# Softmax weights times values in a two-layer decoder trunk: one head at a time over the full width of TensorE, or four heads in a row in the two halves of its columns

## The chip, the core and the metric

The kernel runs on one core of one Trainium2 chip. The metric is device time in microseconds, the median of several executions; lower is better. A profile is taken of one further execution.

## What is computed

A decoder trunk of two layers over 256 tokens with 1024 features, batch 1, all in float32. A layer adds to the stream a mixer of three branches, and then a squared-ReLU MLP with 4096 hidden features:

```python
for l in range(DEPTH):                       # 2
    h = rms_norm(x, attn_norm[l])
    x = x + hybrid_mixer(h, ...)             # MLA, MoBA, retention, gated and merged
    h = rms_norm(x, mlp_norm[l])
    x = x + squared_relu_mlp(h, w_mlp_up[l], w_mlp_down[l])
return rms_norm(x, final_norm)
```

Two of the branches are causal softmax attention with 8 heads, a value dimension of 64 and 256 positions (MoBA's block is as long as the sequence, so only its own causal block remains):

```python
s = jnp.einsum('bhqd,bhkd->bhqk', qb, k) * scale
s = jnp.where(kpos[None, :] <= qpos[:, None], s, NEG_INF)
p = jax.nn.softmax(s, axis=-1)
o = jnp.einsum('bhqk,bhkd->bhqd', p, v)      # the product that the change is about
```

## The kernel before

Tokens are worked on in two tiles of 128. Large products are made from split operands: a value is cut into a rounded part and a rest (`whi`/`wlo` for weights, `xs`, `omlah`/`omlal` and so on for activations), and `three` (L209 to L212) makes three products of them. Weights come in pieces of at most 512 KB over SyncE's queue into four `raw` buffers; ScalarE makes `whi` (L190), VectorE `wlo` (L191).

A layer is a list of units, `prog`: projections, gates, branch products. `at(slot, step)` hangs a further step behind the unit with that number, and `run` goes through the list. What comes of it is the program order; a scheduler then orders each engine's instructions by its own simulated times, except within `tc.manual_schedule`, where the named engine keeps the order in which the code gives them. Engines take their instructions strictly in order.

The attention (`attention`, L433, and `attention_head`, L390) is spread over these slots so that its small steps lie between the large products. Head `h` has three steps: `scores` in slot `first + h`, `turn` two slots later, and `values` three slots later.

- `scores`: query times key into the bank `ps_s`, mask and maximum on VectorE, exponentials on ScalarE, division on VectorE. The result is `prob`, 128 queries by 128 keys and 128 queries by 256 keys. The fourth block of 128x128 is empty by causality and is never made.
- `turn`: three 128x128 transposes on TensorE into `ps_pt` (L421), and a copy on ScalarE to `probT` (L423), which has two buffers: keys on the partitions, queries along the row.
- `values`: two products into `po`, key tile 0 for all 256 queries (L428) and key tile 1 for the last 128 (L429). The stationary operand is 128 columns of the values, which are two heads' 64 columns side by side, so of the 128 rows of the result only the 64 of the head at hand are used.

Two heads share a bank `po`, in its two halves of 256 columns. Behind the odd head's `values`, `out` takes the two useful quarters, rows 0 to 63 of the even head and rows 64 to 127 of the odd one, and splits each with `split_plain`: a copy on ScalarE (L229) and a subtraction on VectorE (L230), 64x256 each. The targets are `omlah`/`omlal` in the MLA branch and `omobah`/`omobal` in the MoBA branch, `oT` in the code, with chunk `i` for the heads `2i` and `2i + 1`. The units `bmla` and `bmoba` multiply them with the branch weights later.

The PSUM banks of `po`, `ps_s`, `ps_pt` and several others come from one pool of four (`misc_tile`). The score products and `values` are plain float32. The values are `vml` in the MLA branch and `mv` in the MoBA branch.

Of the kernel before, what the change touches and what calls it, by code (L numbers as in the profile page):

```python
# [7 lines left out]
F32 = mybir.dt.float32  # L8
# [5 lines left out]
P = 128  # L14
D = 1024
S = 256
# [10 lines left out]
MLA_H, MLA_QR, MLA_KVR, NOPE, ROPE, VD = 8, 256, 128, 64, 32, 64  # L27
QKD = NOPE + ROPE
MB_H, MB_D = 8, 64
# [96 lines left out]
def trunk(ctx: ExitStack, tc: tile.TileContext, x, wts, consts, gains, gfin, xtok, out):  # L126


    nc = tc.nc
# [4 lines left out]
    sb = ctx.enter_context(tc.tile_pool(name="sb", bufs=1))  # L134
# [65 lines left out]
    def misc_tile(name="misc"):  # L200
        return ps.tile([P, 512], F32, name=name, tag="misc", bufs=4)
# [18 lines left out]
    def small(name):  # L220
        return sb.tile([P, 8], F32, name=name, tag="st", bufs=12)
# [6 lines left out]
    def split_plain(src, hi, lo):  # L228
        nc.scalar.activation(hi, src, AF.Copy)  # L229
        nc.vector.tensor_sub(lo, src, hi.bitcast(F32))  # L230
# [154 lines left out]
    def stacked_scores(parts, o, qs, ks, swap=False):  # L385
        for i, (q, k) in enumerate(parts):
            a, b = q[:, qs], k[:, ks]
            nc.tensor.matmul(o, b if swap else a, a if swap else b, start=i == 0, stop=i == 1)  # L388

    def attention_head(o, score, vs, scale):  # L390


        got = {}

        def scores():
            s_ps = misc_tile("ps_s")
            score(s_ps[:, 0:P], slice(0, P), slice(0, P))
            score(s_ps[:, P : 3 * P], slice(P, S), slice(0, S))
            p = sb.tile([P, 3 * P], F32, name="prob", bufs=3)
            m = small("smx")  # L400
            nc.vector.tensor_tensor_reduce(
                p[:, 0:P], s_ps[:, 0:P], mask[:, P : 2 * P], 1.0, NEG_INF, ALU.add, ALU.max, m[:, 0:1]
            )
            nc.vector.tensor_tensor_reduce(
                p[:, P : 3 * P], s_ps[:, P : 3 * P], mask, 1.0, NEG_INF, ALU.add, ALU.max, m[:, 1:2]
            )
            nc.vector.tensor_scalar(m[:, 2:4], m[:, 0:2], -scale, None, op0=ALU.mult)  # L407
            spans = ((0, P), (P, 3 * P))
            for i, (a, b) in enumerate(spans):
                nc.scalar.activation(  # L410
                    p[:, a:b], p[:, a:b], AF.Exp, bias=m[:, 2 + i : 3 + i], scale=scale, accum_out=m[:, 4 + i : 5 + i]
                )
            nc.vector.reciprocal(m[:, 6:8], m[:, 4:6])
            for i, (a, b) in enumerate(spans):
                nc.vector.tensor_scalar(p[:, a:b], p[:, a:b], m[:, 6 + i : 7 + i], None, op0=ALU.mult)
            got["p"] = p

        def turn():
            pt = misc_tile("ps_pt")
            for i, src in enumerate((0, P, 2 * P)):  # L420
                nc.tensor.transpose(pt[:, P * i : P * i + P], got["p"][:, src : src + P], ident)  # L421
            pT = sb.tile([P, 3 * P], F32, name="probT", bufs=2)
            nc.scalar.activation(pT, pt[:, : 3 * P], AF.Copy)  # L423
            got["pT"] = pT

        def values():
            dst, v, pT = o(), vs(), got["pT"]
            nc.tensor.matmul(dst, v[0], pT[:, 0:S], start=True, stop=False)  # L428
            nc.tensor.matmul(dst[:, P:S], v[1], pT[:, S : 3 * P], start=False, stop=True)  # L429

        return scores, turn, values

    def attention(oT, score, vs, scale, first):  # L433


        o_ps = {}

        def o_of(h):
            if h % 2 == 0:
                o_ps[h // 2] = misc_tile("po")  # L440
            return o_ps[h // 2][:, S * (h % 2) : S * (h % 2) + S]

        def out(h):
            i = h // 2
            for j in range(2):
                rows = slice(64 * j, 64 * j + 64)
                split_plain(o_ps[i][rows, S * j : S * j + S], oT[0][rows, i, :], oT[1][rows, i, :])

        for h in range(8):
            steps = attention_head(  # L450
                lambda h=h: o_of(h), lambda o, qs, ks, h=h: score(h, o, qs, ks), lambda h=h: vs(h), scale
            )
            for lag, step in zip((0, 2, 3), steps):
                at(first + h + lag, step)
            if h % 2:
                at(first + h + 3, lambda h=h: out(h))

    def gates(l, key, xn):

# [49 lines left out]
    prog, steps = [], {}  # L509

    def at(slot, step):
        steps.setdefault(slot, []).append(step)

    def slot(key, j):
        return [k for k, _ in prog].index((key, j))
# [9 lines left out]
    def layer(l, xn, before):  # L525

        c0 = []
        c, mla, mqkv, rqkv = {}, {}, {}, {}
# [133 lines left out]
        first = slot("mv", 3)  # L662
        at(first, lambda: omlaT.extend((t4("omlah"), t4("omlal"))))

        def mla_score(h, o, qs, ks):
            nc.tensor.matmul(o, mla["Q"][:, h, qs], mla["K"][:, h, ks], start=True, stop=True)  # L666

        attention(
            omlaT, mla_score,
            lambda h: [v[:, P * (h // 2) : P * (h // 2) + P] for v in mla["v"]], QKD**-0.5, first,  # L670
        )


# [4 lines left out]
        first = slot("gmla1", 3)  # L678
# [12 lines left out]
        for i in range(4):  # L691
            at(first + 2 * i - 1, lambda i=i: moba_turn(i))
        attention(
            omobaT,
            lambda h, o, qs, ks: stacked_scores(qkT[h // 2][h % 2], o, qs, ks),
            lambda h: [v[:, P * (h // 2) : P * (h // 2) + P] for v in mqkv["mv"]], MB_D**-0.5, first,
        )


# [163 lines left out]
        def up(f, between=None):  # L863

            u = misc_tile("pup")
            if f >= NF - WHOLE:
                project_t(l, "up", f, xm, u[:, 0:S])
                return u
            wh, wl = load_w(l, "up", f, 0)
            for k in range(KD):  # L870
                if between and k in between:
                    between[k]()
                nc.tensor.matmul(u, wh[:, k, :], xm.both(k), start=k == 0, stop=False)  # L873
                nc.tensor.matmul(u[:, 0:S], wl[:, k, :], xm.k(k)[0], start=False, stop=k == KD - 1)  # L874
            return u
# [35 lines left out]
        first = [up(f, {1: {4: lambda: xm.stats(accs[3])}, 2: {4: xm.stats_row}}.get(f)) for f in range(LAG + 1)]  # L911
# [20 lines left out]
        if not last:  # L932
# [7 lines left out]
            def turned(q):  # L940
                t, half = quarters[q]
                pt = misc_tile("pyd")
                for i in range(4):
                    nc.tensor.transpose(pt[:, P * i : P * i + P], ys[q][:, P * i : P * i + P], ident)
                x_t = X[half][:, :, P * t : P * t + P]
                nc.vector.tensor_add(x_t, x_t, pt.rearrange("p (k s) -> p k s", k=4))
                xn.take_part(t, half)
# [18 lines left out]
        for t in range(NT):  # L966
            for half in range(2):
                q, cs = 2 * t + half, slice(512 * half, 512 * half + 512)
# [22 lines left out]
    for i, (k, n) in enumerate(b0_units(0)):  # L991
# [4 lines left out]
        tag, bufs = ("t4", T4) if n == 2 else ("w2k", W2K)  # L996
# [22 lines left out]
    for l in range(L):  # L1019
        xn, before = layer(l, xn, before)  # L1020
# [85 lines left out]
```

## Time and profile before

| | us |
|---|---|
| median of 3 executions | 861.49 (861.37 to 861.53) |
| profiled execution | 861.24 |
| its span, first to last instruction of the program | 859.5 |
| TensorE busy (products) | 849.2 |
| TensorE busy (loads of weights) | 728.8 |
| VectorE busy | 618.1 |
| ScalarE busy | 507.7 |

In a row of the profile, PE is TensorE's product, PEld its load of weights, DVE VectorE, ACT ScalarE and SP SyncE. "L428" is the line of the kernel, `po<-probT,vml` the tile written and the tiles read. "128*128" is the part of TensorE's array that a product takes, "128x256" partitions by columns of its result, and "x32" the number of records. A timeline row has the start, the time to the end of the last of its records, and their number. A PE record lasts until its modelled end, so records overlap: what a product costs a full TensorE is the time from its start to the next start. A windows row has the stretch, then the busy time of PE, PEld, DVE, ACT and POOL with instruction counts, the granted clock, and the DMA engines' share and GB/s.

### The profile page before, as it was taken

Reading aid. Unit: us, or ns where it says so; the run is one execution under the profiler, and the core shown is the slowest. Engines: PE = TensorE matmul, PEld = TensorE weight load, DVE = VectorE, ACT = ScalarE, POOL = GpSimd, SP = SyncE. Lnnn points to the kernel's source line nnn. Section 1 sums busy time; section 2 is a strip of 40 time slices with the busy share of each in tenths; the row PEclk is TensorE's granted clock in tenths of the full one; section 3 lists DMA queues with packets and bytes.
Section 4 is the critical chain, followed back from the end, with each engine's and each line's share of the span. In section 5 each row is a group of like instructions: output and inputs, shape, how many; then the busy total and the mean of one; then the engine's idle time right before and its main releaser. Section 6 shows DMA issues by size and latency. Waiting matters only on the chain.

```text
span 859.5 us, 12496 instructions
## 1 busy us (share of the span) xinstructions
PE 849.2 (99%) x4544; PEld 728.8 (85%) x4544; DVE 618.1 (72%) x1198; ACT 507.7 (59%) x885; POOL 12.1 (1%) x23
## 2 busy tenths in 40 slices
PE   8999999999999999999999999999999999999997
PEld 7888888988898888888888888889889988888885
DVE  6896787787777666666589767977877776666664
ACT  7766776535456555555577567665355565555553
POOL 0000000000000000000000000000100000000000
PEclk9999999999999999999999999999999999999999
DMA  9775344446366665555356455445565666666641
GB/s 339 235 233 172 124 147 140 148 155 194 126 196 195 202 192 192 183 188 192 109 202 213 153 159 163 139 140 168 150 194 148 174 205 191 190 182 185 196 123 50
DMA packets 42541, 150.08 MB, mean 175 GB/s; under 512 B 4848, under 2 KB 5360, under 8 KB 42480
## 3 DMA queue, kind: packets, MB, share of 16 engines
q1 hardware_dynamic: 42192, 149.13, 55.7%
q8 instruction: 36, 0.59, 0.3%
q10 hardware_dynamic: 288, 0.16, 0.1%
q14 instruction: 25, 0.20, 0.1%
HBM read 148.22 MB, written 1.05 MB: 174 GB/s over the span
## 4 chain that ended last, share of the span: by engine, by line
PE 96%; DVE 1%; ACT 1%; issue 1%; DMA 1%; SPq 0%; POOLq 0%; POOL 0%; ACTq 0%
PE acc L210 22%; PE acc L211 22%; PE acc L212 22%; PE pup L873 13%; PE pup L874 7%; PE po L428 2%; PE ps_s L666 1%; PE ps_pt L421 1%; PE ps_s L388 1%; PE po L429 1%; DMA raw<-wts 1%; ACT whi L190 0%; PE pqk L686 0%; DVE wlo L191 0%; PE ps_r L388 0%
## 5 line engine op out<-in xcount | busy, mean ns | idle before, releaser
L191 DVE TENSOR_TENSOR wlo<-raw,whi 128x1024 fp32r<-128x1024 f32 (+2 forms) x279 | 336.3, 1209 | 164.2 <-ACT whi L190 162.3
L190 ACT ACTIVATE whi<-raw 128x1024 fp32r<-128x1024 f32 (+2 forms) x279 | 292.0, 1048 | 257.7 <-PE acc L212 152.0
L873 PE MATMUL pup<-xs,whi 128*128 128x512 f32 x496 | 176.9, 398 | 0.0
L211 PE MATMUL acc<-wlo,xs 128*128 128x512 f32 (+1 forms) x384 | 151.8, 395 | 0.6 <-DVE wlo L191 0.6
L210 PE MATMUL acc<-whi,xs 128*128 128x512 f32 (+1 forms) x384 | 150.7, 397 | 0.4 <-ACT whi L190 0.3
L212 PE MATMUL acc<-whi,xs 128*128 128x512 f32 (+1 forms) x384 | 150.7, 393 | 0.0
L874 PE MATMUL pup<-xs,wlo 128*128 128x256 f32 x496 | 138.3, 280 | 0.0
L873 PEld LDWEIGHTS pup<-xs,whi 128*128 128x128 f32 x496 | 92.9, 188 | 21.3
L210 PE MATMUL acc<-whi,sq 128*128 128x512 f32 x256 | 101.5, 397 | 0.4 <-ACT sq L229 0.4
L211 PE MATMUL acc<-wlo,sq 128*128 128x512 f32 x256 | 100.0, 391 | 0.0
L212 PE MATMUL acc<-whi,sq 128*128 128x512 f32 x256 | 99.5, 393 | 0.0
L874 PEld LDWEIGHTS pup<-xs,wlo 128*128 128x128 f32 x496 | 93.6, 189 | 2.2
L210 PEld LDWEIGHTS acc<-whi,xs 128*128 128x128 f32 x384 | 72.2, 188 | 14.3 <-ACT whi L190 1.5
L211 PEld LDWEIGHTS acc<-wlo,xs 128*128 128x128 f32 x384 | 72.3, 188 | 14.1 <-DVE wlo L191 1.6
L212 PEld LDWEIGHTS acc<-whi,xs 128*128 128x128 f32 x384 | 72.3, 188 | 13.0
L212 PEld LDWEIGHTS acc<-whi,sq 128*128 128x128 f32 x256 | 47.9, 188 | 11.7 <-DVE sq L230 0.2
L210 PEld LDWEIGHTS acc<-whi,sq 128*128 128x128 f32 x256 | 48.0, 188 | 11.2 <-ACT sq L229 0.8
L211 PEld LDWEIGHTS acc<-wlo,sq 128*128 128x128 f32 x256 | 48.2, 188 | 8.8
L211 PE MATMUL acc<-mTl,whi 128*128 128x256 f32 x128 | 36.3, 284 | 1.0 <-DVE mTl L230 1.0
L210 PE MATMUL acc<-mTh,whi 128*128 128x256 f32 x128 | 36.2, 285 | 0.0
L212 PE MATMUL acc<-mTh,wlo 128*128 128x256 f32 x128 | 36.1, 283 | 0.0
L410 ACT ACTIVATE prob<-prob,smx 128x128 f32<-128x128 f32 x64 | 28.3, 445 | 7.5 <-DVE smx L407 7.2
(241 smaller groups left out, 1196.3 us busy)
## 6 DMA issues: line engine op xcount, KB each, us to landing
raw<-wts SPq DMA_DIRECT2D x268, 512.0 KB, 3.7
raw<-wts SPq DMA_DIRECT2D x7, 416.0 KB, 3.3
xrow<-xtok SPq DMA_DIRECT2D x4, 256.0 KB, 8.4
y<-y SPq DMA_DIRECT2D x4, 256.0 KB, 2.2
DEC<-consts SPq DMA_DIRECT2D x1, 768.0 KB, 7.5
x<-x SPq DMA_DIRECT2D x1, 512.0 KB, 6.3
raw<-wts SPq DMA_DIRECT2D x2, 256.0 KB, 3.7
gf<-gfin SPq DMA_DIRECT2D x1, 512.0 KB, 3.9
```

What stands on the lines that cost most here:

```text
L190: nc.scalar.activation(hi[:, :sz], raw[:, :sz], AF.Copy)
L191: nc.vector.tensor_sub(lo[:, :sz], raw[:, :sz], hi[:, :sz].bitcast(F32))
L210: nc.tensor.matmul(o, ah, bh, start=start, stop=False)
L211: nc.tensor.matmul(o, ah, bl, start=False, stop=False)
L212: nc.tensor.matmul(o, al, bh, start=False, stop=stop)
L388: nc.tensor.matmul(o, b if swap else a, a if swap else b, start=i == 0, stop=i == 1)
L410: nc.scalar.activation(p[:, a:b], p[:, a:b], AF.Exp, bias=m[:, 2 + i : 3 + i], scale=scale, accum_out=m[:, 4 + i : 5 + i])
L421: nc.tensor.transpose(pt[:, P * i : P * i + P], got["p"][:, src : src + P], ident)
L428: nc.tensor.matmul(dst, v[0], pT[:, 0:S], start=True, stop=False)
L429: nc.tensor.matmul(dst[:, P:S], v[1], pT[:, S : 3 * P], start=False, stop=True)
L873: nc.tensor.matmul(u, wh[:, k, :], xm.both(k), start=k == 0, stop=False)
L874: nc.tensor.matmul(u[:, 0:S], wl[:, k, :], xm.k(k)[0], start=False, stop=k == KD - 1)
```

## The change

`values` is no longer a step of one head. It runs once for four heads, behind the third slot after the last of them; `scores` and `turn` stay per head, where they were. `probT` has five buffers instead of two. `values` takes a bank `po` and makes eight products in it, under `manual_schedule` for TensorE: first the pair of heads 2 and 3 of the four, then heads 0 and 1, and in a pair the odd head and the even one by turns, key tile 0 and then key tile 1. The stationary operand is now the head's own 64 columns. The odd head's result goes to partitions 64 to 127, the even head's to 0 to 63, so a pair fills a half of the bank, 256 columns, and four heads fill it. One `split_plain` over 128x512 then takes the bank to two chunks of `oT`.

```diff
-            pT = sb.tile([P, 3 * P], F32, name="probT", bufs=2)
+            pT = sb.tile([P, 3 * P], F32, name="probT", bufs=5)
             nc.scalar.activation(pT, pt[:, : 3 * P], AF.Copy)
-            got["pT"] = pT
-
-        def values():
-            dst, v, pT = o(), vs(), got["pT"]
-            nc.tensor.matmul(dst, v[0], pT[:, 0:S], start=True, stop=False)
-            nc.tensor.matmul(dst[:, P:S], v[1], pT[:, S : 3 * P], start=False, stop=True)
-
-        return scores, turn, values
+            return pT
+
+        return scores, turn
...
-        o_ps = {}
-
-        def o_of(h):
-            if h % 2 == 0:
-                o_ps[h // 2] = misc_tile("po")
-            return o_ps[h // 2][:, S * (h % 2) : S * (h % 2) + S]
-
-        def out(h):
-            i = h // 2
-            for j in range(2):
-                rows = slice(64 * j, 64 * j + 64)
-                split_plain(o_ps[i][rows, S * j : S * j + S], oT[0][rows, i, :], oT[1][rows, i, :])
+        pT = {}
+
+        def turned(h, turn):
+            pT[h] = turn()
+
+        def values(h0):
+            o, v = misc_tile("po"), vs()
+            with tc.manual_schedule(engines={mybir.EngineType.PE}):
+                for h in (h0 + 2, h0):
+                    cs = slice(S * (h - h0) // 2, S * (h - h0) // 2 + S)
+                    for i in range(2):
+                        for j in (1, 0):
+                            vh = v[i][:, VD * (h + j) : VD * (h + j) + VD]
+                            dst = o[64 * j : 64 * j + 64, cs]
+                            if i == 0:
+                                nc.tensor.matmul(dst, vh, pT[h + j][:, 0:S], start=True, stop=False)
+                            else:
+                                nc.tensor.matmul(dst[:, P:S], vh, pT[h + j][:, S : 3 * P], start=False, stop=True)
+            split_plain(o, *(part[:, h0 // 2 : h0 // 2 + 2, :].rearrange("p k s -> p (k s)") for part in oT))
 
         for h in range(8):
-            steps = attention_head(
-                lambda h=h: o_of(h), lambda o, qs, ks, h=h: score(h, o, qs, ks), lambda h=h: vs(h), scale
-            )
-            for lag, step in zip((0, 2, 3), steps):
-                at(first + h + lag, step)
-            if h % 2:
-                at(first + h + 3, lambda h=h: out(h))
+            scores, turn = attention_head(lambda o, qs, ks, h=h: score(h, o, qs, ks), scale)
+            at(first + h, scores)
+            at(first + h + 2, lambda h=h, turn=turn: turned(h, turn))
+            if h % 4 == 3:
+                at(first + h + 3, lambda h=h: values(h - 3))
```

The two calls of `attention` hand over the two value tiles whole (`lambda: mla["v"]`, `lambda: mqkv["mv"]`) instead of a pair's 128 columns.

More of the change, by code (lines that the diff above doesn't have):

```diff
@@ L388, in stacked_scores, with attention_head @@
             nc.tensor.matmul(o, b if swap else a, a if swap else b, start=i == 0, stop=i == 1)
-    def attention_head(o, score, vs, scale):
+    def attention_head(score, scale):
         got = {}
@@ L669, in layer @@
             omlaT, mla_score,
-            lambda h: [v[:, P * (h // 2) : P * (h // 2) + P] for v in mla["v"]], QKD**-0.5, first,
+            lambda: mla["v"], QKD**-0.5, first,
         )
@@ L695, in layer @@
             lambda h, o, qs, ks: stacked_scores(qkT[h // 2][h % 2], o, qs, ks),
-            lambda h: [v[:, P * (h // 2) : P * (h // 2) + P] for v in mqkv["mv"]], MB_D**-0.5, first,
+            lambda: mqkv["mv"], MB_D**-0.5, first,
         )
```

## The prediction, written before the changed kernel ran

> **What bounds the kernel now.** I read the page first (parts 1 and 4), then the list of who waited for whom on TensorE, then the busy time in the four stretches in which the attention heads run (two layers, two branches).
>
> ```profile
> span 859.5 us, 12496 instructions
> PE 849.2 (99%) x4544; PEld 728.8 (85%) x4544; DVE 618.1 (72%) x1198; ACT 507.7 (59%) x885; POOL 12.1 (1%) x23
> PE 96%; DVE 1%; ACT 1%; issue 1%; DMA 1%; SPq 0%; POOLq 0%; POOL 0%; ACTq 0%
> ```
> ```profile
> PE warm L507 <- DVE zero L152: 1.4, 1, 1.4
> PE acc L211 <- DVE mTl L230: 1.0, 2, 0.5
> PE acc L211 <- DVE wlo L191: 0.6, 1, 0.6
> PE acc L210 <- ACT sq L229: 0.4, 1, 0.4
> PE acc L210 <- ACT whi L190: 0.3, 1, 0.3
> ```
> ```profile
> 57.00:94.00 37.00, 37.00 (x184) 31.13 (x183) 25.43 (x71) 26.14 (x56) 0.00 (x0) 1.00 0.50 160
> 102.00:140.00 38.00, 38.00 (x205) 32.49 (x204) 32.20 (x94) 27.41 (x60) 0.00 (x0) 1.00 0.45 139
> 481.00:518.00 37.00, 37.00 (x183) 31.12 (x182) 25.29 (x72) 25.70 (x56) 0.00 (x0) 1.00 0.52 157
> 526.00:564.00 38.00, 38.00 (x204) 32.50 (x202) 32.22 (x92) 27.92 (x61) 0.00 (x0) 1.00 0.46 139
> ```
>
> The chain that ended last is 96% TensorE. TensorE's waits are 3.7 us in all, and none belongs to the attention (no row names `po`, `ps_s` or `ps_pt`). In the attention stretches TensorE is busy for every microsecond, at full granted clock (1.00), while VectorE has 5.8 us to spare of 38 in its tightest stretch and the DMA engines stand near half. So here a microsecond taken from or added to TensorE's stream moves the end by about a microsecond; the other engines count only if they become late.
>
> **What the product of weights and values costs now.**
>
> ```profile
> 74.32 0.39 PE L210 MATMUL acc<-whi,xs 128*128 128x512 f32 x1
> 74.55 0.39 PE L211 MATMUL acc<-wlo,xs 128*128 128x512 f32 x1
> 74.78 0.59 PE L428 MATMUL po<-probT,vml 128*128 128x256 f32 x2
> 75.21 0.38 PE L429 MATMUL po<-probT,vml 128*128 128x128 f32 x2
> 75.43 0.49 PE L421 MATMUL ps_pt<-K,prob 128*128 128x128 f32 x3
> 75.75 0.82 PE L666 MATMUL ps_s<-KK,Q 128*128 128x128 f32 x4
> 76.22 0.58 PE L212 MATMUL acc<-whi,xs 128*128 128x512 f32 x1
> 76.64 0.39 PE L210 MATMUL acc<-whi,xs 128*128 128x512 f32 x1
> ```
> ```profile
> L428 PE MATMUL po<-probT,vml 128*128 128x256 f32 x32 | 9.5, 377 | 0.0
> L429 PE MATMUL po<-probT,vml 128*128 128x128 f32 x32 | 6.1, 274 | 0.0
> ```
> ```profile
> 74.55 0.41 PEld L428 LDWEIGHTS po<-probT,vml 128*128 128x128 f32 x2
> 74.99 0.40 PEld L429 LDWEIGHTS po<-probT,vml 128*128 128x128 f32 x2
> 75.32 0.36 PEld L421 LDWEIGHTS ps_pt<-K,prob 128*128 128x128 f32 x3
> 75.65 0.53 PEld L666 LDWEIGHTS ps_s<-KK,Q 128*128 128x128 f32 x4
> ```
>
> Each float32 product shows as two passes (x2 in the timeline; 32 records for 16 products of one branch over two layers). What a product costs is start to start: L428 74.78 to 75.21, 0.43 us, so 0.215 a pass; L429 75.21 to 75.43, 0.22, so about 0.108 a pass; a 512-column product of the split weights takes 0.23 (74.32 to 74.55). One head is 0.645 us, four heads 2.58, and the 32 heads (8 heads, 2 branches, 2 layers) 20.6 us. That is all the change can take from: even halved it gives 10.3 us. The 377 ns of a pass is longer than its 0.215 because the results drain for 0.16 us behind it, normally under the next pass.
>
> **The change, part by part.**
>
> *Same passes, narrower.* The number of products stays (8 products, 16 passes, in each of eight groups of four heads), as do their 256 and 128 columns of moving data. Half of the result was unused before: 128 columns of weights, 64 kept. Now 64 columns go to one half of the array. In the built order each group is one unbroken run: odd head, even head (256 columns), odd, even (128 columns), then the other pair. A saving exists only if the halves work at the same time.
>
> Suppose a pass starts as soon as its own half is free and the pass before it has started. Odd head's first pass 0 to 0.215; its second and the even head's first together to 0.43; the even head's second to 0.645, beside both short passes of the odd head; then the even head's two short ones to 0.86. The next pair starts with the last of these, at 0.753, and ends at 1.61. So 1.61 instead of 2.58: **0.97 saved a group, 7.8 in all**. The best case, everything paired, is 1.29 a group: 10.3 saved. From the other side the loads of the weights may set the pace: in the last two PEld rows they follow each other at (0.36 − 0.14)/2 = 0.11 us (a load itself is shown with 0.14 there); 16 loads a group at that pace, if 64 columns load no faster than 128, are 1.76 us: 0.82 saved, 6.6 in all. I take 7.8, since a load of half the columns should not be slower than a full one.
>
> ```profile
> L421 PEld LDWEIGHTS ps_pt<-K,prob x96: 137/142/144, 68.5 to 575.9; 128*128 128x128 f32 x96
> ```
>
> *Sixteen changes of array shape.* Every product of before is 128*128, so no row shows what going to half columns and back costs. Other changes of kind are free: L666 to L212 and on, 75.75 to 76.64, is 0.89 for four passes (0.65) and one 512-column product (0.23). If the array must run empty, the drain of 0.16 is laid open; if besides the next weights cannot be loaded beneath it, another 0.19 (L428's load: 0.41 for two). Bounds 0 and 0.35 a change, 0 to 5.6 us for sixteen; I take the drain alone, **2.6 us added**. The Trainium skill says, in "TensorEngine Tiling (Array Packing)", Key Properties, that changing the tiling mode drains TensorE; the sum by it is that same 2.6, and no row of this trace can bear it out. A gain from the change itself I exclude: the stream is gapless already.
>
> *Evictions.* Before, each pair of heads took two copies on ScalarE and two subtractions on VectorE of 64x256; now four heads take one of each, 128x512.
>
> ```profile
> L229 ACT ACTIVATE omobah<-po x16: 366/378/382, 124.9 to 583.7; 64x256 fp32r<-64x256 f32 x16
> L229 ACT ACTIVATE mTh<-pmt x8: 582/598/602, 221.7 to 652.2; 128x512 fp32r<-128x512 f32 x8
> L230 DVE TENSOR_TENSOR omobal<-po,omobah x16: 409/422/429, 125.8 to 585.0; 64x256 fp32r<-64x256 f32 x16
> L230 DVE TENSOR_TENSOR mTl<-pmt,mTh x8: 680/682/691, 223.0 to 652.8; 128x512 fp32r<-128x512 f32 x8
> ```
>
> With `mTh`/`mTl` as the nearest of that shape, ScalarE goes from 32 × 0.378 to 8 × 0.598 (7.3 us less), VectorE from 32 × 0.422 to 8 × 0.682 (8.0 less). Both lie under a TensorE that never waits for them here: nothing off the end.
>
> *Waits moved.* The first product of a group waits for the last head's `probT`; everything behind it on TensorE waits too. In the built order 18 or more 512-column products stand between that head's transposes and the group, 18 × 0.23 = 4.1 us, against a copy of 0.49 us and perhaps one weight conversion of 1.05 ahead of it:
>
> ```profile
> L423 ACT ACTIVATE probT<-ps_pt x32: 466/490/494, 70.0 to 576.4; 128x384 f32<-128x384 f32 x32
> L190 ACT ACTIVATE whi<-raw 128x1024 fp32r<-128x1024 f32 (+2 forms) x279 | 292.0, 1048 | 257.7 <-PE acc L212 152.0
> ```
>
> Cost nothing; if ScalarE fell over 2.5 us behind there, the rest would be paid up to eight times. The results' consumers (`bmla`, `bmoba`) stand over 40 products behind the last group, some 9 us, against 1.3 us of eviction. Five `probT` buffers hold four heads and one more, and `po` now occupies its bank more briefly. No DMA is issued or moved past by any of it.
>
> **Sum.** 861.24 us is the profiled execution's time (its span 859.5), 0.25 under the median of 861.49. 861.24 − 7.8 + 2.6 = 856.0; against the median 856.3.
>
> **Rivals.**
>
> *The halves do not overlap* (the change does not do what it says). For it: every product here is a float32 one in two passes, and every pass now shown starts after a full pass length. Against: loads and drains already run beside other work. Then four heads still cost 2.58, and only the changes of shape are left: 861.49 + 2.6 = 864.1, between 861.5 and 867.1. It decides on the other side as soon as less than 0.33 us a group overlaps.
>
> *Loads of weights are laid open.* If in half-column form no load runs under a product in flight, all 16 passes of a group pay 0.11 and nothing overlaps: 8 × 1.76 = 14.1 more, 875.6. Against it, the two loads of L428 (74.55 to 74.96) ran while products were under way. The Trainium skill states that rule ("TensorE: Matmul & The Clock Gate", Part 3, What overlaps and what doesn't: a load overlaps only when the row group differs; here all use all rows). By that rule the rows of full width would be impossible, so the trace disagrees.
>
> *The group's first product stalls* on ScalarE, as priced above: 1 us a group gives 861.49 − 5.2 + 8 = 864.3; it eats the gain at 0.65 a group. Against: 4.1 us of cover.
>
> **How the numbers follow.** Overlap 0.70, no overlap 0.18, laid-open loads 0.05, stall 0.07. Predicted is the first, 856.3. Its own range: best 861.49 − 10.3 = 851.2; worst 861.49 − 6.6 + 5.6 = 860.5. The range reaches on to 864.1, the middle of the second case, which leaves out less than 2 in 10. A measurement of this kernel can tell about 0.2%, 1.7 us, from no change. Faster by more: the first case but for its dear end, 0.67. Within: that end and the second case's cheap end, 0.09. Slower: the rest, 0.24.
>
> **What would show it.** Right: in a group, the odd and even heads' passes start together or within a few ns, a group takes 1.6 us from its first start to its last plus a drain, with gaps of about 0.16 ahead of it and behind it, and `PE` has no new wait. Wrong: passes of 64 columns at 0.215 start to start throughout (no overlap); load rows with idle time between passes; a row in which `po` waits for `probT`; or gaps above 0.35 around a group.

## The result and the profile after

The changed kernel takes 853.35 us (853.11 to 853.41 over 4 runs) against 861.51 for the kernel before beside it: ratio 0.9902, 95% interval 0.9889 to 0.9914. That is 8.2 us less, where 5.2 were forecast, within the stated range. The profiled execution's span went from 859.5 to 851.6, 7.9 us.

The page of the changed kernel, span and busy times, and its part 4:

```profile
span 851.6 us, 12430 instructions
PE 840.2 (99%) x4544; PEld 715.8 (84%) x4544; DVE 610.2 (72%) x1174; ACT 499.4 (59%) x861; POOL 12.1 (1%) x23
PE 96%; DMA 1%; DVE 1%; ACT 1%; issue 1%; POOLq 0%; POOL 0%; ACTq 0%
```

The number of TensorE records is the same, 4544; the bound is still TensorE. Who waited for whom on TensorE, changed kernel:

```profile
PE warm L509 <- DVE zero L152: 1.4, 1, 1.4
PE acc L211 <- DVE wlo L191: 1.3, 3, 0.6
PE acc L211 <- DVE mTl L230: 1.0, 2, 0.5
PE acc L210 <- ACT whi L190: 0.8, 1, 0.8
PE acc L210 <- ACT sq L229: 0.4, 1, 0.4
```

Still no row of the attention, so no group stalled for its `probT`; 4.9 us of waits in all, where there were 3.7; the 1.2 us more stand before the large products. The products by shape, and the timeline of the first group of four heads, changed kernel:

```profile
L448 PE MATMUL po<-probT,vml 128*64 128x256 f32 x32 | 5.0, 392 | 0.0
L450 PE MATMUL po<-probT,vml 128*64 128x128 f32 x32 | 3.1, 273 | 0.0
```
```profile
84.18 0.39 PE L211 MATMUL acc<-wlo,xs 128*128 128x512 f32 x1
84.41 0.39 PE L212 MATMUL acc<-whi,xs 128*128 128x512 f32 x1
84.72 0.65 PE L448 MATMUL po<-probT,vml 128*64 128x256 f32 x4
85.20 0.39 PE L450 MATMUL po<-probT,vml 128*64 128x128 f32 x4
85.42 0.60 PE L448 MATMUL po<-probT,vml 128*64 128x256 f32 x4
85.86 0.39 PE L450 MATMUL po<-probT,vml 128*64 128x128 f32 x4
86.17 0.55 PE L421 MATMUL ps_pt<-K,prob 128*128 128x128 f32 x3
86.56 0.28 PE L668 MATMUL ps_s<-KK,Q 128*128 128x128 f32 x1
```

Each row of `po` holds four passes (a float32 product shows as two), two of the odd head and two of the even one. In the second pair the four passes of 256 columns take 85.42 to 85.86, 0.44 us, which is what two such passes took before (0.43): the halves work side by side. One group, start to start, is 84.72 to 86.17, 1.45 us, against 2.58. Around it, L212 lasts 0.31 instead of 0.23, and the three transposes behind it 0.39 (86.17 to 86.56) instead of 0.32. So a group costs 1.45 + 0.08 + 0.07 = 1.60; (2.58 − 1.60) × 8 = 7.8 us, near the span's 7.9. The match is good to about a microsecond only, since the 1.2 us of waits are not in the sum and the order of the products around the heads moved as well.

The loads of weights in the same group:

```profile
84.72 0.20 PEld L448 LDWEIGHTS po<-probT,vml 128*64 128x64 f32 x4 [0.35 <-ACT whi L190]
84.99 0.36 PEld L450 LDWEIGHTS po<-probT,vml 128*64 128x64 f32 x4
85.32 0.25 PEld L448 LDWEIGHTS po<-probT,vml 128*64 128x64 f32 x4
85.64 0.36 PEld L450 LDWEIGHTS po<-probT,vml 128*64 128x64 f32 x4
86.17 0.31 PEld L421 LDWEIGHTS ps_pt<-K,prob 128*128 128x128 f32 x3 [0.17 <-issue]
```

At the group's start the loads had been idle for 0.35 us and come at the same time as the first product (84.72), where the loads of L428 began ahead of theirs (74.55 against 74.78): at this change of array shape no load was taken ahead. (The row names ScalarE as releaser. But the product ahead takes the same 0.31 to 0.32 us at every one of the eight groups, and with full-width products in the same places, the first experiment below, it takes 0.23, 84.86 to 85.09; so it is the change of shape.) Within the group loads run under products of both halves.

### The profile page after: what moved, and what is told of

Same layout as the page of the kernel before. It is cut to its first block, busy times and chain, and to the rows that moved or that the text cites. A ratio compares the mean times of both kernels' runs of the same rounds, so it can differ in the third digit from the quotient of the medians.

```text
span 851.6 us, 12430 instructions
## 1 busy us (share of the span) xinstructions
PE 840.2 (99%) x4544; PEld 715.8 (84%) x4544; DVE 610.2 (72%) x1174; ACT 499.4 (59%) x861; POOL 12.1 (1%) x23
## 4 chain that ended last, share of the span: by engine, by line
PE 96%; DMA 1%; DVE 1%; ACT 1%; issue 1%; POOLq 0%; POOL 0%; ACTq 0%
PE acc L210 22%; PE acc L212 22%; PE acc L211 22%; PE pup L875 14%; PE pup L876 7%; PE ps_pt L421 1%; PE ps_s L668 1%; PE po L448 1%; DMA raw<-wts 1%; PE ps_s L388 1%; ACT whi L190 0%; PE po L450 0%; PE pqk L688 0%; DVE wlo L191 0%; PE ps_r L388 0%
## 5 line engine op out<-in xcount | busy, mean ns | idle before, releaser
L211 PE MATMUL acc<-wlo,xs 128*128 128x512 f32 (+1 forms) x384 | 150.2, 391 | 1.3 <-DVE wlo L191 1.3
L212 PE MATMUL acc<-whi,xs 128*128 128x512 f32 (+1 forms) x384 | 149.5, 390 | 0.0
L211 PE MATMUL acc<-wlo,sq 128*128 128x512 f32 x256 | 100.0, 391 | 0.0
L212 PE MATMUL acc<-whi,sq 128*128 128x512 f32 x256 | 99.5, 393 | 0.0
L211 PEld LDWEIGHTS acc<-wlo,xs 128*128 128x128 f32 x384 | 72.2, 188 | 14.8 <-DVE wlo L191 2.2
L212 PEld LDWEIGHTS acc<-whi,xs 128*128 128x128 f32 x384 | 72.2, 188 | 13.6 <-issue 0.3
L212 PEld LDWEIGHTS acc<-whi,sq 128*128 128x128 f32 x256 | 47.9, 188 | 11.7 <-DVE sq L230 0.2
L211 PEld LDWEIGHTS acc<-wlo,sq 128*128 128x128 f32 x256 | 48.2, 188 | 8.7
L211 PE MATMUL acc<-mTl,whi 128*128 128x256 f32 x128 | 36.3, 284 | 1.0 <-DVE mTl L230 1.0
L212 PE MATMUL acc<-mTh,wlo 128*128 128x256 f32 x128 | 36.1, 283 | 0.0
```

Of the source, the lines that this page charges most:

```text
L211: nc.tensor.matmul(o, ah, bl, start=False, stop=False)
L212: nc.tensor.matmul(o, al, bh, start=False, stop=stop)
```

## Experiments

**Is it the overlap, the grouping or the lighter evictions?** First, the changed kernel's places and buffers with the full-width products and the evictions of before:

```diff
-            o, v = misc_tile("po"), vs()
+            os, v = [misc_tile("po") for _ in range(2)], vs()
...
                 for h in (h0 + 2, h0):
... (the eight products of the changed kernel and its one eviction go)
+                    o, vs2 = os[(h - h0) // 2], [t[:, VD * h : VD * h + P] for t in v]
+                    for j in (1, 0):
+                        dst = o[:, S * j : S * j + S]
+                        nc.tensor.matmul(dst, vs2[0], pT[h + j][:, 0:S], start=True, stop=False)
+                        nc.tensor.matmul(dst[:, P:S], vs2[1], pT[h + j][:, S : 3 * P], start=False, stop=True)
+            for h in range(h0, h0 + 4):
+                rows, j = slice(64 * (h % 2), 64 * (h % 2) + 64), h % 2
+                o = os[(h - h0) // 2]
+                split_plain(o[rows, S * j : S * j + S], oT[0][rows, h // 2, :], oT[1][rows, h // 2, :])
```

The four heads need two banks here, and the products go head by head, as before.

> Four heads in a row as in the changed kernel, in the same slots and with five probT buffers, but each product with 128 columns of weights over the full width and the evictions of before (four quarters of 64x256). Theory A: neither grouping nor buffers give anything, 861.5 within 1 us, ratio 1.000. Theory B1 (the grouping is what saves, by fewer interruptions of the large products): near 853 to 857.

Measured 861.41 us, ratio 0.9996 (0.9987 to 1.0006). Grouping and buffers give nothing.

Second, the changed kernel with the evictions in quarters:

```diff
-            split_plain(o, *(part[:, h0 // 2 : h0 // 2 + 2, :].rearrange("p k s -> p (k s)") for part in oT))
+            for h in range(h0, h0 + 4):
+                rows = slice(64 * (h % 2), 64 * (h % 2) + 64)
+                cs = slice(S * ((h - h0) // 2), S * ((h - h0) // 2) + S)
+                split_plain(o[rows, cs], oT[0][rows, h // 2, :], oT[1][rows, h // 2, :])
```

> The changed kernel, but a group's bank is evicted in four quarters of 64x256 as before (some 7 us more of ScalarE and 8 us more of VectorE in all). Theory A: they lie under TensorE, 853.4 within 1 us, ratio 0.990 to 0.991. Theory B2 (the lighter evictions give part of the gain): up to 8 us slower, 855 to 861.

Measured 853.63 us, ratio 0.9906 (0.9891 to 0.9921), as the changed kernel. The busy times of this kernel:

```profile
PE 841.1 (99%) x4544; PEld 716.8 (84%) x4544; DVE 617.5 (73%) x1198; ACT 506.4 (59%) x885; POOL 12.1 (1%) x23
```

VectorE works 7.3 us more than in the changed kernel and ScalarE 7.0, and neither shows in the time.

**Is a narrow product cheaper by itself?** The kernel before, one head at a time, with the head's own 64 columns:

```diff
-            return o_ps[h // 2][:, S * (h % 2) : S * (h % 2) + S]
+            j = h % 2
+            return o_ps[h // 2][64 * j : 64 * j + 64, S * j : S * j + S]
...
-            lambda h: [v[:, P * (h // 2) : P * (h // 2) + P] for v in mla["v"]], QKD**-0.5, first,
+            lambda h: [v[:, VD * h : VD * h + VD] for v in mla["v"]], QKD**-0.5, first,
... (and the same for `mqkv["mv"]` in the MoBA branch)
```

> The kernel before with one edit: a head's two products take its own 64 columns of the values and write its own 64 rows, so they run in half of the array, but still one head at a time, with the schedule and evictions of before. Theory A (half-width products are as slow as full ones; each stretch of them costs two changes of shape, 0.305 us a stretch as read from the changed kernel's trace): 32 stretches, 9.8 us more, 871.3, ratio 1.011. Theory D (a half-width product is itself cheaper, and that is the gain): 861.5 - 10.3 + 9.8 = 861, ratio 1.000 or below.

Measured 871.66 us, ratio 1.0114 (1.0099 to 1.0129): 10.0 us slower. Timeline around one head:

```profile
75.28 0.39 PE L211 MATMUL acc<-wlo,xs 128*128 128x512 f32 x1
75.59 0.65 PE L428 MATMUL po<-probT,vml 128*64 128x256 f32 x2
76.08 0.38 PE L429 MATMUL po<-probT,vml 128*64 128x128 f32 x2
76.39 0.55 PE L421 MATMUL ps_pt<-K,prob 128*128 128x128 f32 x3
76.77 0.82 PE L667 MATMUL ps_s<-KK,Q 128*128 128x128 f32 x4
```

L211 takes 0.31 to the next start instead of 0.23, L428 0.49 instead of 0.43, L429 0.31 instead of 0.22, the transposes 0.38 instead of 0.32: some 0.3 us for a stretch of half-width work (an unbroken run of such products), and nothing gained. So half-width products without a partner lose, by 10.0/32 = 0.31 us a stretch.

**Does the price scale with the number of stretches?** Two heads in a row (with three `probT` buffers and evictions of 128x256), and all eight (with two banks, nine buffers and `W2K = 15`, two row tiles fewer, to make room). Of each, the line that places the products:

```diff
-            if h % 4 == 3:
-                at(first + h + 3, lambda h=h: values(h - 3))
... (two heads)
+            if h % 2:
+                at(first + h + 3, lambda h=h: values(h - 1))
... (eight heads)
+            if h == 7:
+                at(first + h + 3, lambda: values(0))
```

> The changed kernel with two heads in a row instead of four: 16 stretches instead of 8, three probT buffers, evictions of 128x256. Theory A (all overlaps within a pair, 10.3 us saved, 0.305 a stretch): 861.5 - 10.3 + 4.9 = 856.1, ratio 0.9937. Theory E (the changes of shape cost next to nothing and the 0.305 is a matter of the stretch's neighbours): 853.5, ratio 0.9906.

Measured 856.30 us, ratio 0.9939 (0.9924 to 0.9954).

> All eight heads of a branch in a row: 4 stretches instead of 8, two banks, nine probT buffers; the pool of 2 KB row tiles goes from 17 to 15 to make room. Theory A: 861.5 - 10.3 + 1.2 = 852.4, ratio 0.9895, about 1.2 us under the changed kernel. Rival: the two row tiles that are gone, or the results that come later, make TensorE wait and eat it: 853.5 or more; the next kernel shows the first of these alone.

Measured 852.00 us (851.59 to 853.08), ratio 0.9889 (0.9874 to 0.9903).

The control, the changed kernel with `W2K = 15`:

> The changed kernel with 15 row tiles instead of 17, and nothing else: the control of the kernel with eight heads. If two tiles fewer cost nothing: 853.4, ratio 0.9906. If they cost, the difference is their price.

Measured 853.42 us (853.21 to 853.88), ratio 0.9905 (0.9889 to 0.9922): two row tiles fewer cost nothing. With 16, 8 and 4 stretches the times are 856.3, 853.4 and 852.0: 0.36 us a stretch in both steps, near the 0.31 of single heads. The traces say the same: from its first start to the next product's, a stretch of two, four and eight heads takes 0.81 (75.62 to 76.43), 1.45 and 2.75 us (103.47 to 106.22). Two heads more add about 0.65, what one head took before, and the rest does not grow with the length. Theory E falls. Eight heads in a row is the fastest version measured; the ratios' intervals overlap with four heads, but the runs themselves do not (851.59 to 853.08 against 853.21 to 853.88 of the control).

**Must the halves alternate?** Two other orders of the same eight products. Halves in blocks of four:

```diff
-                for h in (h0 + 2, h0):
-                    cs = slice(S * (h - h0) // 2, S * (h - h0) // 2 + S)
-                    for i in range(2):
-                        for j in (1, 0):
+                for j in (1, 0):
+                    for h in (h0 + 2, h0):
+                        cs = slice(S * (h - h0) // 2, S * (h - h0) // 2 + S)
+                        for i in range(2):
```

> The changed kernel with the eight products of a group in another order: first the four of the two odd heads (all in the upper half of the columns), then the four of the even heads. Widths, schedule slots and evictions stay. Theory A (the gain is the two halves working at once, and needs products of both halves next to each other): hardly anything overlaps, only the changes of array shape remain, 16 x 0.15 us = 2.4: 863.9 us, ratio to before about 1.003; a group takes about 2.6 us start to start. Theory B (the gain comes from the grouping of four heads or from the larger evictions): as the changed kernel, 853.4, ratio 0.990. Theory C (TensorE looks far ahead and finds the other half's products itself): also 0.990, and odd and even passes start together.

Head by head, blocks of two:

```diff
-                    for i in range(2):
-                        for j in (1, 0):
+                    for j in (1, 0):
+                        for i in range(2):
```

> The changed kernel with a pair's products head by head: odd head key tile 0, key tile 1, then the even head's two, so the halves change every two products instead of every one. Theory A in the strict form (a pass starts only when the pass before it in order has started and its own half is free): three short overlaps of 0.11 us a group, 0.32 x 8 = 2.6 us saved, 2.4 spent on the changes of shape: 861.3, ratio 1.000. Theory C (TensorE takes up products of the other half ahead of their turn): 853.4, ratio 0.990. Something between tells how far it looks.

Blocks of four: 859.12 us, ratio 0.9972 (0.9960 to 0.9983). Blocks of two: 853.92 us, ratio 0.9908 (0.9893 to 0.9923). Theory A in both forms was too strict: blocks of two lose nothing that the times can tell (in the trace a group takes 1.50 us, 84.92 to the transposes at 86.42, instead of 1.45), and blocks of four still gain 2.7 us. Theory C without a limit falls with the blocks of four. The timeline of the blocks of four:

```profile
84.51 0.65 PE L448 MATMUL po<-probT,vml 128*64 128x256 f32 x2
84.99 0.38 PE L450 MATMUL po<-probT,vml 128*64 128x128 f32 x2
85.21 0.65 PE L448 MATMUL po<-probT,vml 128*64 128x256 f32 x4
85.64 0.44 PE L450 MATMUL po<-probT,vml 128*64 128x128 f32 x4
85.91 0.59 PE L448 MATMUL po<-probT,vml 128*64 128x256 f32 x2
86.34 0.38 PE L450 MATMUL po<-probT,vml 128*64 128x128 f32 x2
86.66 0.55 PE L421 MATMUL ps_pt<-K,prob 128*128 128x128 f32 x3
```

Passes 1 to 8 belong to the odd heads, 9 to 16 to the even ones. The first four stand alone (x2, x2), then eight run in pairs (x4, x4), then four alone. The even half's first pass, the ninth in order, starts with the odd half's fifth. And with head by head, the even half's first pass, the fifth in order, starts with the first, four passes in the time of two:

```profile
84.92 0.66 PE L448 MATMUL po<-probT,vml 128*64 128x256 f32 x4
85.40 0.40 PE L450 MATMUL po<-probT,vml 128*64 128x128 f32 x4
```

From these two I formed a rule: each half takes its own passes in order, and a pass may start once the pass four places before it has started. A third order, not used to form it, tries it:

```diff
-                for h in (h0 + 2, h0):
+                for j, h, i in (
+                    (1, h0 + 2, 0), (1, h0 + 2, 1), (1, h0, 0), (0, h0 + 2, 0),
+                    (0, h0 + 2, 1), (0, h0, 0), (1, h0, 1), (0, h0, 1),
+                ):
... (the two inner loops go, and the body stays)
```

> The changed kernel with a group's eight products in the order three odd, three even, one odd, one even. Theory C4 (each half takes its own passes in order, and a pass may start as soon as the pass four places before it has started; read from the two reordered kernels): the even half starts with the odd half's third pass, a group takes 1.92 us from its first start to the next product's, 0.51 us a group saved against before: 857.4, ratio 0.9952. If the reach were unlimited: 853.4, 0.9906. If only a neighbouring pass could overlap: about 861, 0.999.

Measured 857.63 us, ratio 0.9955 (0.9938 to 0.9972). Its timeline:

```profile
84.20 0.65 PE L449 MATMUL po<-probT,vml 128*64 128x256 f32 x2
84.68 0.27 PE L451 MATMUL po<-probT,vml 128*64 128x128 f32 x1
84.69 0.43 PE L449 MATMUL po<-probT,vml 128*64 128x256 f32 x1
84.79 0.27 PE L451 MATMUL po<-probT,vml 128*64 128x128 f32 x1
...
86.13 0.55 PE L421 MATMUL ps_pt<-K,prob 128*128 128x128 f32 x3
```

The L449 pass at 84.69 is the seventh in order and starts with the third (84.68), ahead of the fourth (84.79); the group takes 84.20 to 86.13, 1.93 us, where the rule gave 1.92. A record does not name its half; that the pass is the even head's is read from its line, its place, and its 0.43 us instead of 0.38, which in this group only the odd half's first pass shows besides.

## Why the prediction was right, and what was off

- *What bounds it*: right. Microseconds taken from TensorE's stream came off the end (7.8 worked out from one group, 7.9 of span, to within the microsecond said above). That 7.8, what is left after the changes of shape, equals the forecast's 7.8 for the overlap alone by chance.
- *The overlap*: the mechanism was right, its size was off. Predicted 7.8 us, with 10.3 as the best case; the trace shows the best case: a group's 1.45 us is 1.29, all passes paired, and 0.16 that does not grow with the length of the stretch and so belongs to the two changes of shape. The step that failed is "a pass starts as soon as its own half is free and the pass before it has started". The two passes of an odd head's product do not hold the even head back: its first pass, third in order, starts with the odd head's first, and the reordered kernels show such a start up to four places ahead. The kernel's description has engines take their instructions strictly in order; for products in the two halves of TensorE these traces show otherwise. So nothing of a group runs alone in the built order, where the forecast had the first pass, the last ones and the seam between the pairs alone.
- *The bound by loads*: the 1.76 us a group was too dear. The 0.11 us between loads that it rests on is the pace of the products they served (0.108 a pass of 128 columns), so it was no bound of the loads themselves. And loads of the two halves run side by side: the four of L448 at 84.72 take 0.20 us, where at 0.11 apart they would take 0.14 + 3 × 0.11 = 0.47. A whole group is done in 1.45.
- *The changes of shape*: predicted 0.16 each and 2.6 us in all. Measured 0.31 to 0.36 a stretch, so 0.16 to 0.18 each and 2.5 to 2.9 for sixteen. The size was right, the make-up only in part. The product behind a change starts 0.08 to 0.09 us late, not 0.16 (L212 takes 0.31 instead of 0.23, the last L450 0.31 instead of 0.22 for such a row). Besides, the first pass behind each change is slower: 0.27 us until the next in its half, the 0.65 of the row at 84.72 less the last record's 0.38, instead of 0.215. Its load is seen not to be taken ahead; that this is the reason is likely, not shown. The Trainium skill's rule ("TensorEngine Tiling (Array Packing)", Key Properties) that a change of tiling mode drains TensorE agrees with these late starts. That TensorE ran empty they do not show: the first product of the group starts (84.72) before the modelled end of the one ahead (84.41 + 0.39).
- *Evictions*: nothing off the end, as said. The single eviction saves VectorE 7.3 us and ScalarE 7.0 against quarters in the same kernel, where 8.0 and 7.3 were forecast.
- *Waits moved*: no stall on `probT`, as said.
- *Rivals*: no overlap is out by the trace; laid-open loads by the load rows within a group; a stall by the list of waits. The Trainium skill's rule that loads overlap only between different row groups ("TensorE: Matmul & The Clock Gate", Part 3, What overlaps and what doesn't) is not borne out here either. Nor is what the same section of the Trainium skill says of products, that they start and end in program order: in the last timeline a product of the other half starts ahead of the three passes before it.

What stays open: whether the reach is four passes or two products (each float32 product here is two passes, so these runs cannot tell), why the first pass behind a change of shape is slower, and what the reach is for other types.

## What to carry to other kernels

Where TensorE is the bound and a product uses half the columns, two such products in the two halves cost one here. Each stretch of them costs about 0.3 us for the changes of shape, so collect them: single heads lost 10.0 us here, stretches of two, four and eight heads gained 5.4, 8.2 and 9.7. Change halves after at most two products: blocks of two gained nearly as much as strict alternation, while an order that began with three of one half gained 4.0 us and blocks of four 2.7.

## What the runs showed that I had not expected

Within a stretch, TensorE started a pass of the other half ahead of up to three passes that stood before it, together with the pass four places before it and no earlier. And float32 passes in the two halves each keep their full rate (0.215 us for 256 columns, both at once), with their loads running under them.
